# A fp32 decoder trunk on one core: weight tiles split once and kept in DRAM scratch, instead of split for every token group

## The chip, the core and the metric

The kernel runs on one core of a Trainium2 chip. The metric is the device time of one execution in microseconds (us). The engines are TensorE (PE), which multiplies matrices, VectorE (DVE), ScalarE (ACT), GpSimd (POOL), and SyncE (SP), from whose queue this kernel issues all of its DMAs, in order.

## The reference

One layer of a hybrid decoder trunk, for 2048 prompt tokens and 8 sample rows (one new token each for 8 sequences with state and caches), width 1024, all in float32. Cut to what matters:

```python
h    = rmsnorm(x, ln_mix)
proj = h @ w_in                      # 1024 x 3592
# A: gated DeltaNet, 4 heads x 128 (short convolution, chunked recurrence, gated norm) -> od
# B: dilated window attention, 8 heads x 64, three branches (window, dilation), ALiBi      -> oa
x    = x + concat(od, oa) @ w_out    # 1024 x 1024
h    = rmsnorm(x, ln_ffn)
x    = x + square(relu(h @ w_ffn_up)) @ w_ffn_down   # 1024 x 4096, 4096 x 1024
y    = rmsnorm(x, ln_final)
```

The outputs are y, the convolution's and the recurrence's last states, and the caches of keys and values, those of the samples shifted by one row (a copy of 64 MB).

## The kernel before, in words

**Dense products.** The 2056 tokens are worked in four groups (0 to 511, 512 to 1023, 1024 to 1535, and 1536 to 2055 in two pieces of 260). A float32 product is made of three: both operands are split, x = hi + lo with both parts in fp32r, and hi·hi, hi·lo and lo·hi are summed in PSUM (`dense`, L234, matmul at L244). A weight tile is 128 × 1024 floats (512 KB): 24 matmuls of 512 columns for a group (48 of 260 in the last). There are 100 such tiles: 28 of the input projection (`win`), 8 of the output projection (`wout`), 32 of the MLP's upper matrix (`wup`), 32 of its lower one (`wdn`). Each group goes through all of them, and the last takes 4 tiles of `wdn` twice, which makes 404 loads.

**A weight tile's way.** `load_w` (L219) issues the DMA of the raw tile from SP (L223), into a ring of `self.ahead` = 3 buffers; ACT copies it to `whi`, which rounds it (L216), and POOL subtracts that from the raw tile, which gives `wlo` (L217); `whi` and `wlo` have rings of three. When the mixers are done, `late` (L1474, called when the second group's MLP ends) opens a new pool of weights and sets `self.ahead` to 5.

**Order of the work.** First `in_proj` for the four groups, whose results are drained from PSUM by DVE and ACT, convolved, and stored to DRAM scratch from SP (`d_dn<-ct`, L382 and L390, for the recurrence's inputs; others for queries, keys and values). Then `ffn` (L1412): `out_proj` of the first group, and for each group the MLP, with the next group's `out_proj` before its last eighth. Beside the dense products run the *mixers*, a generator (`all_mixers`, L1266) which makes one step for every 10 dense products: recurrence inputs of the first half of the tokens (`delta_first(0)`, L527 to L569, each of 8 chunks ending in the PE line L569); the inverses of the recurrence's blocks (`dn_blocks`, L588 and L590, 31 steps of two DVE instructions for each half) beside the first half's attention; the scan over its chunks (`delta_scan(0)`, L627 to L729); then `delta_first(1)`, `dn_blocks(1)`, `attention(1)` (scores L840 and L866, transposes L822, products with the values L850 and L879, softmax on DVE L806 and ACT L810), `delta_scan(1)` and the sample rows. Before each `out_proj` the mixers are drained up to what it needs.

The program writes these as they come; a scheduler then sets each engine's fixed order, by priorities: what supplies the dense products first (lane "feed"), then the mixers, then the dense products (L31). The caches' copies (`copy_piece`, L1431, 128 of 512 KB, DRAM to DRAM) are spread over 300 weight tiles, from the 40th on. At the start the first group's tokens come as `xs`, are normed in parts (`s<-xs,cols`, L285), and the first row scale `rb` (L212) is made from their squares.

Of the kernel before, what the change touches and what calls it, by code (L numbers as in the profile page):

```python
# [7 lines left out]
F32 = mybir.dt.float32  # L8
# [8 lines left out]
T = 2048            # prompt tokens  # L17
NB = 8              # sample rows
TT = T + NB
# the token ranges of the dense products  # L20
GROUPS = (((0, 512),), ((512, 512),), ((1024, 512),), ((1536, 260), (1796, 260)))
# those of the first norm, the first group in parts so that the products start early
# [5 lines left out]
# weight tiles after which, and over which, the copies of the caches are spread  # L28
COPY_FROM, COPY_UNITS = 40, 300
COPY_LANE, COPY_LAG = 'mixer', 1  # L30
# dense products of 512 columns to a step of the mixers, beside the input projection and beside the MLP  # L31
STEPS = 10, 10
# blocks of queries between the scores and the turn, and between the turn and the products with the values
# [3 lines left out]
class Build:  # L37
    def __init__(self, nc, tc, ctx, I, O):
# [10 lines left out]
        self.pace = []  # L49
        self.units = -COPY_FROM  # L50
# [5 lines left out]
    # ---------------------------------------------------------------- helpers  # L56
    def stage(self, i):
        """Within a stage an engine prefers what keeps the dense products supplied, then the
        small products of the mixers, then the dense products, which fill what is left."""
        self.lanes = {k: 1000 + i * 1000000 + n * 300000 for n, k in enumerate(("feed", "mixer", "dense"))}  # L60
# [9 lines left out]
    def mix_step(self):  # L70
        """The next step of the mixers; TensorE takes it up after the dense products emitted so far."""
        with self.lane("mixer"), self.tc.issue_after(self.last), self.tc.issue_after(self.last_v):
            if next(self.mixers, None) is None:
                self.mixers = None

    def advance(self, products):
        """Called after so many dense products of 512 columns."""
        self.credit += products
        while self.credit >= self.step:
            self.credit -= self.step  # L80
            if self.mixers is not None:
                self.mix_step()

    def next_later(self):
        """A step of each generator of self.later, behind the dense products emitted so far."""
# [20 lines left out]
    def consts(self):  # L106
# [24 lines left out]
        # q is scaled by 1 / (8 slope) of its head, a power of two  # L131
# [5 lines left out]
    def scratch(self):  # L137
# [14 lines left out]
        self.d_s = dr.tile([16, 4096], F32, name="d_s")  # L152
        self.d_S = dr.tile([128, 512], F32, name="d_S")
# [11 lines left out]
    def rsqrt(self, y, v, t):  # L165
        """y = v ** -0.5 for v > 0."""
# [9 lines left out]
    def sumsq(self, x, n, k, tmp, tag):  # L176
        """Adds the squares of x, the k-th of eight tiles, to self.acc."""
# [9 lines left out]
    def rms_steps(self, out, n, tmp):  # L187
        """Leaves 1 / rms of n tokens in the rows of out, from self.acc. In steps."""
# [25 lines left out]
    def split(self, hi, lo, x, eng):  # L214
        """x = hi + lo, exactly up to the rounding of lo to float32r."""
# [3 lines left out]
    def load_w(self, src):  # L219
        nc, W = self.nc, self.W  # L220
        with self.lane("feed"):
            raw = W.tile([128, 1024], F32, name="wraw", bufs=self.ahead)
            ins = nc.sync.dma_start(raw, src)  # L223
            hi, lo = [W.tile([128, 1024], F32R, name=n) for n in ("whi", "wlo")]
            self.split(hi, lo, raw, nc.gpsimd)
# [8 lines left out]
    def dense(self, w, wo, hi, lo, off, n, p=None):  # L234
        """PSUM bank with sum_k w[k].T @ act[k][:, off:off+n]; both operands are split in two and the
        product of the low parts is below float32's last place."""
# [14 lines left out]
    # ---------------------------------------------------------------- input projection  # L251
    def norm1(self, g, X, nx):
        """Splits of x ln; the rows of rb hold 1 / rms of the tokens, by which the products are scaled. In steps."""
# [5 lines left out]
        for i, (c0, n) in enumerate(NORM1[g]):  # L259
# [10 lines left out]
            if g == 0:  # L270
                if i == 0:
                    self.w0 = [self.load_w(I["win"][4])]
# [4 lines left out]
                if i == 0:  # L277
                    self.w0 += [self.load_w(I["win"][u]) for u in (5, 6)]
# [4 lines left out]
    def norm_split(self, hi, lo, x, ln):  # L283
        """hi + lo = x ln"""
# [3 lines left out]
    def in_proj(self, g, following=None):  # L288
# [8 lines left out]
        for kind, j in order:  # L297
# [11 lines left out]
            else:  # L309
                units = [(self.load_w(I["win"][first[kind] + j]), j)]  # L310
            for c0, n in pieces:
                for w, i in units:
                    # the mixers' banks are free while the first scales are awaited
# [17 lines left out]
    def unit_ba(self, g, hi, lo):  # L331
        """Projections to beta and the decay: the weight's high part in columns 0..7, its low part in 32..39."""
# [21 lines left out]
    def silu2(self, y, n):  # L354
        """silu(2 y)"""
# [6 lines left out]
    def scaled(self, out, p, c0, n, scale=1.0):  # L362
        """out = p scale / rms of the tokens from c0"""
# [61 lines left out]
    def turn_values(self, y, j, c0, np_):  # L425
        """The values with the tokens on the partitions."""
# [18 lines left out]
    # ------------------------------------------------------- gates and DeltaNet  # L445
    def gate_math(self, pool, b, a, n, beta, g):
        """beta = sigmoid(b); g = -exp(a_log) * softplus(a + dt_bias); b, a: [128, n, 4] views."""
# [57 lines left out]
    def dn_first(self, c):  # L505
        """Everything of a chunk that does not depend on the state."""
# [11 lines left out]
        # decay[j, (h, i)] = exp(gc_i - gc_j) for i >= j, else 0  # L518
# [22 lines left out]
        # cc = beta / |k|^2, 1/|k| -> |k|  # L541
# [34 lines left out]
    def dn_blocks(self, half):  # L576
        """Inverses of the 32 x 32 unit upper triangular diagonal blocks, one block to a partition."""
# [18 lines left out]
    def dn_inverse(self, c, out):  # L596
        """Loads a chunk and completes the inverse of its unit upper triangular matrix."""
# [25 lines left out]
        # 32 -> 64  # L623
# [22 lines left out]
        # 64 -> 128  # L646
# [13 lines left out]
    def dn_scan(self, c, nak, x, u):  # L660
        """Takes the state through a chunk and leaves the chunk's outputs."""
# [75 lines left out]
    def together(self, *gens):  # L737
        """Runs generators side by side, a step of each at a time."""
# [32 lines left out]
    # ---------------------------------------------------------------- attention  # L771
    def attn_consts(self):
        nc, A = self.nc, self.A
        # -(distance in positions) of query p from key kk of (previous block, own block), -BIG outside the band
# [10 lines left out]
        # the widest branch: queries 64.. of each of two residues, keys 0..127 of its residue  # L785
# [6 lines left out]
        # row 6 part + 2 branch + head gives its value to the 64 rows of the head, for its branch  # L792
# [7 lines left out]
    def attn_softmax(self, j, b):  # L800
        """exp(score - max) of a block of queries for the two heads, with -max and the sums."""
# [11 lines left out]
    def attn_turn(self, b):  # L813
        """The block's probabilities with the keys on the partitions."""
# [17 lines left out]
    def attn_wide(self, hf, qd, i, qr, ks, so):  # L832
        """Scores of two residues of the widest branch."""
# [20 lines left out]
    def attn_near(self, br, hf, qd, i, parts, ks, so):  # L854
        """Scores of 128 queries of a near branch."""
# [27 lines left out]
    def attn_load(self, j, hf):  # L883
        """The queries of a head twice, its keys' high and low parts: (q, q) . (k high, k low) = q . k"""
# [41 lines left out]
    def attn_blocks(self, hf):  # L926
        """For each block of queries its scores, and what to do with its probabilities."""
# [59 lines left out]
    def attention(self, half):  # L987
        while self.have_at < 2 * half + 2:
            yield 1
        with self.pool(f"A{half}", 2, side="right") as self.A:  # L990
# [3 lines left out]
            while True:  # L994
                # a step: the products of one block, the turn of a later one, the scores of a still later one
# [16 lines left out]
    def attn_combine(self, j, t, s0, o):  # L1012
        """Weighs the branches' outputs for 512 tokens from t by their softmax denominators."""
# [6 lines left out]
        # e: exp(branch max - max), then the weights; columns 2 branch + head  # L1020
# [36 lines left out]
    # ---------------------------------------------------------------- sample rows  # L1057
    def sample_dn(self):
# [14 lines left out]
        # norms of q and k; kq[., bh, 0] = k, kq[., bh, 1] = q  # L1073
# [11 lines left out]
        # gates, the same on all partitions, in the order (b, h)  # L1085
# [9 lines left out]
        # state products  # L1095
# [446 lines left out]
```

## Time and profile before

| | us |
|---|---|
| median of 3 runs | 3205.29 (3204.25 to 3205.44) |
| span of the profiled execution | 3203.3 |
| PE, DVE, ACT, POOL busy | 2980.6, 2019.5, 1149.1, 1105.9 |
| start and the first of the input projection | 0 to 210 |
| rest of it, beside the first half's recurrence inputs and attention | 210 to 880 |
| first scan | 880 to 1160 |
| second half's inputs and block inverses, as the MLP of the first group goes on | 1160 to 1310 |
| second attention | 1310 to 1760 |
| second scan and the sample rows | 1760 to 2200 |
| dense products alone | 2200 to 3203 |

The span of the profiled execution is its own time from the first to the last recorded instruction; the median of the runs is 2.0 us above it. A line of the profile names a line of the code, the engine, the operation with its output and inputs, the shape, the count, the busy time, the mean of one in ns, and the engine's idle time before it with what ended it. The stages above have soft edges, since the mixers run beside the dense products.

### The profile page before, as it was taken

Reading aid. Unit: us, or ns where it says so; the run is one execution under the profiler, and the core shown is the slowest. Engines: PE = TensorE matmul, PEld = TensorE weight load, DVE = VectorE, ACT = ScalarE, POOL = GpSimd, SP = SyncE. Lnnn points to the kernel's source line nnn. Section 1 sums busy time; section 2 is a strip of 40 time slices with the busy share of each in tenths; the row PEclk is TensorE's granted clock in tenths of the full one; section 3 lists DMA queues with packets and bytes.
Section 4 is the critical chain, followed back from the end, with each engine's and each line's share of the span. In section 5 each row is a group of like instructions: output and inputs, shape, how many; then the busy total and the mean of one; then the engine's idle time right before and its main releaser. Section 6 shows DMA issues by size and latency. Waiting matters only on the chain.

```text
span 3203.3 us, 47999 instructions
## 1 busy us (share of the span) xinstructions
PE 2980.6 (93%) x17793; PEld 2489.5 (78%) x17793; DVE 2019.5 (63%) x4502; ACT 1149.1 (36%) x2298; POOL 1105.9 (35%) x557
## 2 busy tenths in 40 slices
PE   8898889999989889999999988979999999999997
PEld 6677667778988667677777767767888888999997
DVE  8658878657777687655546676685546344465545
ACT  4333335555523332344445332212233223332223
POOL 3333332232232234222223322424334444444443
PEclk9999999999989989999999988989999999999998
DMA  4555775455465665544444644675335444332222
GB/s 144 168 184 171 242 212 160 140 153 169 132 191 176 191 203 195 162 130 131 124 118 145 206 150 163 215 227 200 129 112 184 133 140 162 119 112 93 93 93 67
DMA packets 349321, 499.52 MB, mean 156 GB/s; under 512 B 74904, under 2 KB 247416, under 8 KB 343968
## 3 DMA queue, kind: packets, MB, share of 16 engines
q1 hardware_dynamic: 349088, 496.46, 50.4%
q8 instruction: 141, 2.31, 0.3%
q14 instruction: 92, 0.75, 0.1%
HBM read 414.61 MB, written 148.93 MB: 176 GB/s over the span
## 4 chain that ended last, share of the span: by engine, by line
PE 56%; DVE 12%; DMA 3%; issue 2%; ACT 1%; SPq 0%; POOL 0%; DVEq 0%; ACTq 0%; POOLq 0%
PE dense L244 44%; PE bank L866 2%; PE bank L822 2%; PE bank L879 1%; PE bank L840 1%; DVE y L1404 1%; PE bank L671 1%; DMA ak<-d_kl 1%; DVE s L1387 1%; DVE tmp L1386 1%; DVE dt L172 1%; DVE drr L173 1%; DVE racc L185 1%; PE bank L688 1%; PE bank L673 1%
## 5 line engine op out<-in xcount | busy, mean ns | idle before, releaser
L244 PE MATMUL dense<-s,whi 128*128 128x512 f32 (+2 forms) x8000 | 1702.6, 357 | 36.3 <-DVE y L1404 10.4
L217 POOL TENSOR_TENSOR wlo<-wraw,whi 128x1024 fp32r<-128x1024 f32 x404 | 979.7, 2425 | 1740.7 <-ACT whi L216 816.6
L244 PEld LDWEIGHTS dense<-s,whi 128*128 128x128 f32 x8000 | 1310.9, 192 | 252.5 <-issue 26.4
L244 PE MATMUL dense<-s,wlo 128*128 128x512 f32 (+2 forms) x4000 | 893.9, 356 | 0.0
L244 PEld LDWEIGHTS dense<-s,wlo 128*128 128x128 f32 x4000 | 664.3, 191 | 106.8 <-issue 6.5
L216 ACT ACTIVATE whi<-wraw 128x1024 fp32r<-128x1024 f32 x404 | 427.0, 1057 | 854.7 <-PE dense L244 707.7
L1404 DVE TENSOR_TENSOR y<-dense,y 128x512 f32<-128x512 f32 (+1 forms) x320 | 185.6, 583 | 295.5 <-PE dense L244 295.0
L1386 DVE TENSOR_TENSOR tmp<-tmp 128x512 f32<-128x512 f32 (+1 forms) x160 | 197.7, 1236 | 68.9 <-ACT s L1385 68.8
L810 ACT ACTIVATE as<-as,as 128x256 f32<-128x256 f32 (+2 forms) x384 | 169.9, 444 | 180.5 <-DVE as L806 170.9
L806 DVE CUSTOM_DVE_ANT_0 as<-bank,nd 128x256 f32<-128x256 f32 (+2 forms) x384 | 122.7, 349 | 160.9 <-PE bank L866 106.9
L1383 DVE SCALAR_TENSOR_TENSOR tmp<-dense,rb 128x512 f32<-128x512 f32 (+1 forms) x160 | 93.3, 583 | 172.7 <-PE dense L244 171.1
L1385 ACT ACTIVATE s<-tmp 128x512 fp32r<-128x512 f32 (+1 forms) x160 | 87.6, 548 | 292.1 <-DVE tmp L1383 290.7
L379 DVE SCALAR_TENSOR_TENSOR cy<-cr,cw,cy 128x512 f32<-128x512 f32 (+3 forms) x189 | 151.8, 804 | 12.2 <-ACT cy L377 10.1
L822 PE MATMUL bank<-ident,as 128*128 128x128 f32 (+1 forms) x600 | 112.1, 289 | 5.3 <-ACT as L810 4.0
L1387 DVE TENSOR_TENSOR s<-tmp,s 128x512 fp32r<-128x512 f32 (+1 forms) x160 | 107.6, 672 | 4.1
L822 PEld LDWEIGHTS bank<-ident,as 128*128 128x128 f32 (+1 forms) x600 | 65.0, 138 | 36.7 <-issue 17.8
L866 PE MATMUL bank<-ak,aql 128*128 128x256 f32 x256 | 88.2, 356 | 1.2 <-DVE aql L217 1.2
L866 PE MATMUL bank<-ak,aqh 128*128 128x256 f32 x256 | 88.4, 357 | 0.0
L358 ACT ACTIVATE ct<-cy 128x512 f32<-128x512 f32 (+3 forms) x83 | 44.1, 532 | 119.6 <-DVE cy L379 85.5
L827 DVE COPY apt<-bank 128x512 f32<-128x512 f32 (+2 forms) x96 | 55.3, 576 | 48.1 <-PE bank L822 43.9
L840 PE MATMUL bank<-ak,aq 128*64 128x64 f32 (+1 forms) x512 | 73.5, 374 | 12.7 <-issue 8.4
L879 PE MATMUL bank<-apt,av 128*64 128x128 f32 x944 | 82.9, 288 | 0.0
(343 smaller groups left out, 2871.7 us busy)
## 6 DMA issues: line engine op xcount, KB each, us to landing
wraw<-wdn SPq DMA_DIRECT2D x132, 512.0 KB, 3.6
wraw<-wup SPq DMA_DIRECT2D x128, 512.0 KB, 3.5
wraw<-win SPq DMA_DIRECT2D x112, 512.0 KB, 4.1
s_wk<-ck SPq DMA_DIRECT2D x64, 511.8 KB, 5.4
s_wv<-cv SPq DMA_DIRECT2D x64, 511.8 KB, 5.9
d_nak<-nak SPq DMA_DIRECT2D x16, 1024.0 KB, 4.8
nak<-d_nak SPq DMA_DIRECT2D x16, 1024.0 KB, 6.1
wraw<-wout SPq DMA_DIRECT2D x32, 512.0 KB, 3.9
```

The lines of the kernel that those rows point to most:

```text
L216: self.nc.scalar.activation(hi, x, AF.Copy)
L217: return eng.tensor_tensor(out=lo, in0=x, in1=hi, op=OP.subtract)
L244: self.last = nc.tensor.matmul(p[:, :n], a[:, wo + k * 128:wo + (k + 1) * 128], x[k][:, off:off + n], start=i == 0 and k == 0, stop=i == 2 ...
L379: nc.vector.scalar_tensor_tensor(y[:, :np_], r[:, i:i + np_], self.cw[:, j, i:i + 1], y[:, :np_], op0=OP.mult, op1=OP.add)
L806: nc.vector.tensor_tensor_reduce(out=st[:, hh, :nk], in0=b["s"][hh], in1=b["nd"], op0=OP.add, op1=OP.min, scale=-(2.0 ** -(2 * j + hh + 1) ...
L810: nc.scalar.activation(st[:, hh, :nk], st[:, hh, :nk], AF.Exp, bias=so[:, i, hh:hh + 1], scale=-1.0, accum_out=so[:, i, 2 + hh:3 + hh])
L822: nc.tensor.transpose(pT[:m, w * 128:(w + 1) * 128], b["p"][:, hh, kb * 128:kb * 128 + m], self.ident)
L866: nc.tensor.matmul(p[:, 256 * hh:256 * hh + 256], x[:, q], ks[hh][:, k], start=n == 0, stop=n == 1)
L879: self.nc.tensor.matmul(po[s64, 128 * i:128 * i + 128], v[:, own - (nkb - 1 - kb) * step, s64], b["pt"][:, hh * nkb + kb, :], start=kb == ...
L1386: nc.vector.tensor_tensor(out=u[:, :n], in0=u[:, :n], in1=u[:, :n], op=OP.mult)
L1387: nc.vector.tensor_tensor(out=ul[:, s], in0=u[:, :n], in1=uh[:, s], op=OP.subtract)
L1404: self.last_v = nc.vector.tensor_tensor(out=y[m][:, s], in0=p[:, :n], in1=y[m][:, s], op=OP.add).ins
```

## The change: the split tiles are kept

The parts of a weight tile are worked out when it is first needed (the first group), and stored to a DRAM scratch of 100 tiles of 1 MB, `d_w`. The other 304 loads bring both parts at once, by one DMA of 1 MB, and need neither ACT nor POOL. The two parts lie in one tile `w` with a ring of `self.ahead` buffers; the raw tile has a ring of 3.

```diff
+        self.kept = {}
...
+        self.d_w = dr.tile([100, 128, 2, 1024], F32, name="d_w")
...
-    def load_w(self, src):
+    def load_w(self, name, *i):
         nc, W = self.nc, self.W
+        again = (name, *i) in self.kept
+        k = self.kept.setdefault((name, *i), len(self.kept))
         with self.lane("feed"):
-            raw = W.tile([128, 1024], F32, name="wraw", bufs=self.ahead)
-            ins = nc.sync.dma_start(raw, src)
-            hi, lo = [W.tile([128, 1024], F32R, name=n) for n in ("whi", "wlo")]
-            self.split(hi, lo, raw, nc.gpsimd)
+            both = W.tile([128, 2, 1024], F32R, name="w", bufs=self.ahead)
+            hi, lo = both[:, 0], both[:, 1]
+            if again:
+                ins = nc.sync.dma_start(both.bitcast(F32), self.d_w[k])
+            else:
+                raw = W.tile([128, 1024], F32, name="wraw", bufs=3)
+                ins = nc.sync.dma_start(raw, self.I[name][i])
+                self.split(hi, lo, raw, nc.gpsimd)
+                nc.sync.dma_start(self.d_w[k], both.bitcast(F32))
...
-                units = [(self.load_w(I["win"][first[kind] + j]), j)]
+                units = [(self.load_w("win", first[kind] + j), j)]
```

The other callers name their tiles in the same way: ("wout", u), ("wup", f), ("wdn", c, m // 2). In the changed kernel a line stands 10 further down than before (2 further ahead of `load_w`): the matmul of the dense products is L254 there, the load of the kept parts L230, the raw load L233, the store L235.

The change also moves instructions, since the scheduler orders them anew. First PE, where the second attention begins. Before (`dense` are the dense products, L840 scores, L822 transposes of the probabilities, L850 products with the values):

```order
L244 MATMUL dense<-s,whi 128x512 x16
L244 MATMUL dense<-s,wlo 128x512 x6
L840 MATMUL bank<-ak_12809,aq_12808 64x128 x4
L244 MATMUL dense<-s,wlo 128x512 x2
L244 MATMUL dense<-s,whi 128x512 x16
L244 MATMUL dense<-s,wlo 128x512 x8
L244 MATMUL dense<-s,whi 128x512 x8
L244 MATMUL dense<-s,wlo 128x512 x4
```

Now, from the last chunk of the recurrence's inputs on (L537 to L579; L850 are the scores here, L832 the transposes, L860 the products with the values):

```order
L254 MATMUL dense<-s,w 128x512 x170
L537 MATMUL bank<-ident,dx 128x128 x4
L540 MATMUL bank<-ident,dx 128x128 x4
L563 MATMUL bank<-ident,dx 128x128 x4
L568 MATMUL bank<-dx 128x128 x4
L579 MATMUL bank<-dx 128x128 x4
L254 MATMUL dense<-s,w 128x512 x188
L850 MATMUL bank<-ak_12474,aq_12473 64x128 x4
L850 MATMUL bank<-ak_12480,aq_12479 64x128 x4
L832 MATMUL bank<-ident,as 128x128
L850 MATMUL bank<-ak_12474,aq_12473 64x128
L832 MATMUL bank<-ident,as 128x128
```

Before, 890 dense products stand among those of the second attention. Now none does: all of it stands in one piece behind them, and each chunk of the second half's recurrence inputs in one piece too, with 170 to 190 dense products between two chunks. Also four or five of the eight chunks of the first scan stand without dense products between them, where some 60 stood.

Next SP, in the input projection of a later group (`d_dn<-ct` is a store of a drained tile, the `nak` rows are stores of the recurrence's inputs). Before:

```order
L382 DMA d_dn<-ct 128x512
L223 DMA wraw<-win 128x1024
L574 DMA d_blk<-nak 32x4x32 x4
L571 DMA d_nak<-nak 128x2048
L382 DMA d_dn<-ct 128x512
L223 DMA wraw<-win 128x1024
L574 DMA d_blk<-nak 32x4x32
L382 DMA d_dn<-ct 128x512
L223 DMA wraw<-win 128x1024
```

Now:

```order
L392 DMA d_dn<-ct 128x512
L230 DMA w<-d_w 128x2048
L584 DMA d_blk<-nak 32x4x32 x3
L392 DMA d_dn<-ct 128x512
L584 DMA d_blk<-nak 32x4x32
L230 DMA w<-d_w 128x2048
L581 DMA d_nak<-nak 128x2048
L392 DMA d_dn<-ct 128x512
L230 DMA w<-d_w 128x2048
```

The rows alternate in the same way. What moved is which tile a load is for: before, the raw load of a tile stood behind the store of the drained product six or seven tiles earlier; now the load of the kept parts stands behind that of four tiles earlier, sometimes three.

Last ACT, at the start (L285 and L295 norm a part of the tokens, L184 and L186 square it, L212 and L214 make the row scale `rb`). Before:

```order
L216 ACTIVATE whi<-wraw 128x1024
L285 ACTIVATE s<-xs,cols 128x256
L184 ACTIVATE ct<-xs 128x256
L285 ACTIVATE s<-xs,cols 128x256
L184 ACTIVATE ct<-xs 128x256
L285 ACTIVATE s<-xs,cols 128x256 x8
L181 ACTIVATE racc<-xs 128x256
```

Now:

```order
L295 ACTIVATE s<-xs,cols 128x256
L186 ACTIVATE ct<-xs 128x256
L214 ACTIVATE rb<-fbank 128x256
L387 ACTIVATE cy<-cr,cw 128x256 x2
L218 ACTIVATE w<-wraw 128x1024
L295 ACTIVATE s<-xs,cols 128x256 x5
L183 ACTIVATE racc<-xs 128x256
```

The copy of the third weight tile, and the norm of the second half of the first tokens behind it, stand behind the first row scale now; before they stood ahead of it. On SP the first two stores of kept parts stand ahead of that half's loads.

More of the change, by code (lines that the diff above doesn't have):

```diff
@@ L271, in norm1 @@
                 if i == 0:
-                    self.w0 = [self.load_w(I["win"][4])]
+                    self.w0 = [self.load_w("win", 4)]
                 for k in range(8):
@@ L277, in norm1 @@
                 if i == 0:
-                    self.w0 += [self.load_w(I["win"][u]) for u in (5, 6)]
+                    self.w0 += [self.load_w("win", u) for u in (5, 6)]
             yield 1
@@ L1316, in out_proj @@
         for u in range(8):
-            w = self.load_w(I["wout"][u])
+            w = self.load_w("wout", u)
             with self.lane("feed"):
@@ L1375, in up @@
         g0 = GROUPS[g][0][0]
-        w = self.load_w(I["wup"][f])
+        w = self.load_w("wup", f)
         uh, ul = self.stile(), self.stile()
@@ L1399, in down @@
             if m % 2 == 0 and (c0 == g0 or (c == 7 and g == 3)):
-                w = self.load_w(I["wdn"][c, m // 2])
+                w = self.load_w("wdn", c, m // 2)
             s = slice(c0 - g0, c0 - g0 + n)
```

## The prediction

> **What bounds the kernel now.** I read the page's totals and its chain of waits first, then busy time by stretches of the span, then the waits of TensorE (PE) and of SyncE's queue (SP).
>
> ```profile
> span 3203.3 us, 47999 instructions
> PE 2980.6 (93%) x17793; PEld 2489.5 (78%) x17793; DVE 2019.5 (63%) x4502; ACT 1149.1 (36%) x2298; POOL 1105.9 (35%) x557
> ...
> PE 56%; DVE 12%; DMA 3%; issue 2%; ACT 1%; SPq 0%; POOL 0%; DVEq 0%; ACTq 0%; POOLq 0%
> ```
>
> PE is busy 93% of the span, so 3203.3 − 2980.6 = 222.7 us is all that is idle; after PE the chain goes by VectorE (DVE), and GpSimd (POOL) and ACT, whose weight work the change removes, hold hardly any of it themselves. The stretches (columns: us, then busy time and count of PE, PEld, DVE, ACT, POOL, then granted clock, DMA share, GB/s) show where the idle time lies:
>
> ```profile
> 0.00:210.00 210.00, 180.40 (x808) 147.22 (x809) 135.46 (x262) 81.06 (x133) 76.85 (x36) 0.95 0.53 162
> 210.00:880.00 670.00, 625.32 (x3864) 504.61 (x3863) 493.75 (x1351) 313.98 (x765) 204.93 (x108) 0.98 0.58 173
> 880.00:1160.00 280.00, 244.42 (x1866) 217.86 (x1865) 203.68 (x488) 90.98 (x195) 78.47 (x54) 0.91 0.61 183
> 1160.00:1310.00 150.00, 133.74 (x629) 107.05 (x628) 122.97 (x287) 39.13 (x53) 59.50 (x40) 0.97 0.59 194
> 1310.00:1760.00 450.00, 437.17 (x2633) 334.38 (x2632) 237.01 (x715) 213.87 (x561) 120.08 (x61) 0.99 0.49 134
> 1760.00:2200.00 440.00, 382.68 (x2110) 308.97 (x2110) 316.72 (x646) 110.97 (x195) 139.41 (x82) 0.91 0.59 188
> 2200.00:3203.00 1003.00, 976.89 (x5895) 869.42 (x5893) 509.94 (x759) 299.08 (x398) 426.66 (x181) 0.99 0.38 125
> ```
>
> PE is idle 45 us beside the first attention (210 to 880), 36 and 57 us beside the two scans (880 to 1160, 1760 to 2200), where the granted clock is 0.91, and only 13 us beside the second attention (1310 to 1760) and 26 us in the last third. The waits by name:
>
> ```profile
> PE bank L729 <- DVE dw L724: 50.4, 14, 6.5
> ...
> PE dense L244 <- ACT whi L216: 9.5, 3, 7.4
> ```
>
> The largest is a small product of the scan that waits for a DVE result. The dense products wait for a split weight 3 times, 9.5 us in all: weights are not what is late now.
>
> **The change part by part.** *What goes.* Of 404 weight tiles 304 are loaded ready-made.
>
> ```profile
> L217 POOL TENSOR_TENSOR wlo<-wraw,whi 128x1024 fp32r<-128x1024 f32 x404 | 979.7, 2425 | 1740.7 <-ACT whi L216 816.6
> ...
> L216 ACT ACTIVATE whi<-wraw 128x1024 fp32r<-128x1024 f32 x404 | 427.0, 1057 | 854.7 <-PE dense L244 707.7
> ```
>
> That is 304 × 2.425 = 737 us of POOL and 304 × 1.057 = 321 us of ACT. Both engines are idle some 2000 us, so by itself this is worth nothing. What it does to DVE is another matter. Two answers of the timeline, DVE's and POOL's, of the same moment (start, duration):
>
> ```profile
> 1292.31 0.39 DVE L590 TENSOR_TENSOR bu<-bu,bt 128x220 f32<-128x220 f32 x1
> 1292.73 2.60 DVE L588 TENSOR_TENSOR bt<-bn,bu 128x207 f32<-128x207 f32 x1
> 1295.37 0.37 DVE L590 TENSOR_TENSOR bu<-bu,bt 128x207 f32<-128x207 f32 x1
> ...
> 1292.72 2.39 POOL L217 TENSOR_TENSOR wlo<-wraw,whi 128x1024 fp32r<-128x1024 f32 x1 [6.11 <-ACT whi L216]
> ```
>
> A DVE instruction of 0.37 us lasts 2.60 us when it starts beside the subtraction: 2.2 us lost. The Trainium skill (SBUF — State Buffer, section "SBUF: two separate sides") says that the port pair shared by the two engines is an exclusive lock held for a whole instruction, its loser blocked; the trace agrees, 2.60 beside 0.37 us. The price lies between 0 (the subtraction falls into DVE's idle time) and 304 × 2.2 = 669 us of DVE time; DVE is busy 63%, so I take about half, some 330 us. Little of it bounds PE: it is 10% of the span, and the idle time before PE that DVE can end is that of the first attention and the two scans, 45 + 36 + 57 = 138 us. I take a third, **−45 us**, between −90 and −10.
>
> *Start.* The ACT order changes: the third copy and the later norm copies now stand behind the row scale.
>
> ```profile
> 14.69 1.04 ACT L216 ACTIVATE whi<-wraw 128x1024 fp32r<-128x1024 f32 x1
> ...
> 28.77 0.38 ACT L212 ACTIVATE rb<-fbank 128x256 f32<-128x256 f32 x1 [1.55 <-PE fbank L209]
> ```
>
> SP also has two stores, which wait for POOL, ahead of the second half of the tokens, so that half is normed later. The row scale stands 14 us behind this weight copy, the tokens' order in it is what shifts; where the products of the tiles at hand cover it, nothing is lost. From 0 to 12 us, about half taken: **+7 us**.
>
> *Stores.* 100 stores of 1 MB join the first group's loads. A store waits on SP for POOL's subtraction, and behind it stand the next loads of raw tiles and stores of the projection; but the raw loads waited for that subtraction before, too, for their slot. So the price is in the bytes.
>
> ```profile
> DMA packets 349321, 499.52 MB, mean 156 GB/s; under 512 B 74904, under 2 KB 247416, under 8 KB 343968
> ...
> q1 hardware_dynamic: 349088, 496.46, 50.4%
> ...
> s_wk<-ck SPq DMA_DIRECT2D x64, 511.8 KB, 5.4
> ...
> dx<-d_dn SPq DMA_DIRECT2D x16, 768.0 KB, 5.6
> ```
>
> ```profile
> 2240.00:2320.00 80.00, 80.00 (x346) 64.67 (x345) 39.62 (x45) 23.45 (x29) 31.71 (x14) 1.00 0.40 132
> 2400.00:2480.00 80.00, 80.00 (x353) 64.97 (x352) 51.10 (x65) 28.82 (x38) 37.93 (x16) 1.00 0.56 188
> ```
>
> At a share of 0.56 the engines moved 188 GB/s, so full they would move 188 / 0.56 = 336. In the first group's MLP a tile means 0.52 MB raw, 1.05 MB stored, a share of the cache copies (128 of 0.52 MB over 300 tiles, 0.22) and of the recurrence's traffic (8 chunks of 0.79 MB of dx and 1.05 MB of nak over some 52 tiles, 0.28): 2.07 MB, 6.2 us. A dense tile takes 24 × 80 / 346 = 5.55 us, and with a tenth of small products 6.15 us. DMA and PE come out level, so queueing decides: between 0 and 0.3 us on each of 100 tiles, **+10 us** (0 to 30). By the Trainium skill's measured 425 GB/s for one core (DMA: Bandwidth & Descriptors, section "Bandwidth") 2.07 MB would take an estimated 4.9 us, and this term would be 0.
>
> *Weights later.* Loads of the later groups go straight into a ring of three tiles (five in the last two groups), which a tile leaves only when its last product is done. Before, raw tiles ran ahead of that; now the lead is two tiles, 2 × 5.55 = 11.1 us, less the landing. SP, in order, has them behind stores of the projection (where it waits for DVE), and had waited for POOL instead.
>
> ```profile
> SPq L223 <- POOL wlo L217: 1481.6, 332, 22.9
> ```
> ```profile
> wraw<-wup SPq DMA_DIRECT2D x128, 512.0 KB, 3.5
> ...
> d_nak<-nak SPq DMA_DIRECT2D x16, 1024.0 KB, 4.8
> nak<-d_nak SPq DMA_DIRECT2D x16, 1024.0 KB, 6.1
> ```
>
> Nearest to a 1 MB load is the 1 MB of nak, 4.8 to 6.1 us, which leaves 5 us. So it is mostly covered; where SP stands behind a late store it isn't. **+8 us**, from 0 to 40 (304 tiles, one in ten 1.3 us late).
>
> *Second attention bare.* On PE the end of the recurrence's inputs and the second attention, spread among 890 dense products before, now stand bare behind them.
>
> ```profile
> L244 PE MATMUL dense<-s,whi 128*128 128x512 f32 x649 | 178.5, 406 | 0.0
> L244 PE MATMUL dense<-s,wlo 128*128 128x512 f32 x328 | 95.1, 408 | 0.0
> ```
> ```profile
> 1337.40:1374.60 37.20, 37.20 (x274) 27.97 (x273) 16.97 (x75) 22.66 (x75) 2.37 (x1) 1.00 0.47 136
> ```
>
> Between 1310 and 1760 us stand 649 + 328 = 977 dense products, 977 × 0.231 = 226 us, and so 2633 − 977 = 1656 small ones in some 217 us, 0.131 us each. Their work is the same; the price is the waits that nothing fills. The stretch of 37 us has 274 products of 0.136 us, so nearly all of them small, and PE is busy through all of it at full clock: 0 is the lower end inside the attention. At its start a chain is bare but for the 188 dense products ahead of it:
>
> ```profile
> 1256.92 4.31 DMA bn<-d_blk
> ...
> 1310.47 8.45 DMA ak<-d_kl
> ```
> ```profile
> L588 DVE TENSOR_TENSOR bt<-bn,bu x62: 190/372/2603, 416.3 to 1303.8; 128x31 f32<-128x31 f32 x4, 128x60 f32<-128x60 f32 x4, 128x87 f32<-128x87 f32 x4, 128x112 f32<-128x112 f32 x4
> ```
>
> A store near 4 us, this load of 4.3, 62 DVE steps of 0.37 (23 us, 35 with other DVE work between), a store again, then 8.45 for the keys: 45 to 60 us, beside 188 × 0.231 = 43. About 10 us are idle there, 5 more at each of three changes of heads, up to a tenth of 217 us for bare chains, and 10 us where the clock falls, as it did to 0.91 beside idle stretches: some 57 less the 13 us idle there before, **+45 us**, from 10 to 110 (a quarter of 217 us bare, and a chunk or two of recurrence besides).
>
> Sum: 3203.3 − 45 + 7 + 10 + 8 + 45 = 3228.3 us of span. The median of the runs (3205.29) is 2.0 us above this execution's span, so I add 2: **3230 us**.
>
> **Rivals.** *DVE's relief decides (faster).* Every removed subtraction that a DVE instruction of a chain now meets gives back the 2.2 us of the row. If the relief reaches its −90, the attention keeps PE full as in the 37 us row (+15), and the stores and start cost +12 and weights 3, the time is 3205 − 90 + 30 = 3145 to 3180 with less; I give **3172**. The Trainium skill's rule above, an exclusive lock, stands behind this rival. For it speaks that DVE is 82% busy beside the second blocks (122.97 of 150 us); against it, that it has to gain on PE, idle 7%.
>
> *The DMAs decide (slower by much).* The bytes rise from 499.52 MB by 100 × 1.05 written and 304 × 0.52 read, to 763. In this stretch the share is already 0.78 and PE loses its pace:
>
> ```profile
> 320.00:400.00 80.00, 66.64 (x340) 55.24 (x340) 64.97 (x161) 30.23 (x50) 29.76 (x18) 0.91 0.78 242
> ```
>
> If a tile's load comes later than the 5 us to spare (a landing above 11 us, or SP held 5 us by a store), each such tile shows it whole. With 100 of 304 tiles 0.6 us late (60) and the stores at +30, the time is 3230 + 52 + 20 = **3302**. Against: the share over the span would be only 50.4 × 763 / 499.52 = 77%.
>
> *Nothing to be measured.* Runs of this kernel lie within about 1 us; I call 0.2% (6.4 us) the least that can be told from no change. Relief at −65 and the rest as forecast give 3210.
>
> **How the numbers follow.** Forecast, slower by 0.2 to 2.5%: 0.40. Relief: 0.31. DMAs: 0.17. No change: 0.12. So faster 0.31, same 0.12, slower 0.57. Terms at their kind ends (−90, 10 and 0s) give 3125, at their bad ends (−10, 12, 30, 40, 110) 3387, which need not come together; a tenth left out on either side, the range goes from 3160 to 3310.
>
> **What would show it.** Right: DVE instructions of 2.6 us in the recurrence's steps are gone after the first group; PE has 30 to 80 us idle in the second attention; dense products wait for a weight load a few us in all, and where SP holds one back behind a projection's store. Wrong: PE idle under 20 us in the bare attention (then faster), or waits of dense products for the weight loads above 60 us (then slower).

## The result, and the profile after

The changed kernel takes 3226.47 us (median of 5 runs, 3223.65 to 3228.29), the kernel before in the same session 3205.29 (3202.89 to 3208.72): the ratio is 1.0061, 95% interval 1.0044 to 1.0077. It is slower by some 20 us, near the forecast of 3230. But that the sum came out right is luck: large errors of opposite sign in it cancelled, as the experiments show.

The page's totals after:

```profile
span 3221.5 us, 47130 instructions
PE 2969.5 (92%) x17793; PEld 2479.9 (77%) x17793; DVE 1707.0 (53%) x4502; ACT 834.6 (26%) x1994; POOL 365.3 (11%) x253
...
q1 hardware_dynamic: 363488, 760.71, 71.8%
```

DVE has 2019.5 − 1707.0 = 312 us less to do with the same 4502 instructions, POOL 741 and ACT 315 us less. PE is busy 11 us less, but idle 3221.5 − 2969.5 = 252 us instead of 223. The stretches, cut where PE's own stages end in this kernel (same columns as before):

```profile
0.00:240.00 240.00, 198.28 (x876) 158.65 (x877) 135.46 (x275) 83.97 (x139) 69.98 (x34) 0.94 0.76 272
240.00:876.00 636.00, 625.04 (x3833) 503.70 (x3831) 384.68 (x1346) 241.68 (x689) 33.54 (x37) 0.99 0.79 241
876.00:1215.00 339.00, 287.21 (x2037) 250.79 (x2036) 211.49 (x504) 89.42 (x194) 70.21 (x49) 0.91 0.77 246
1215.00:1530.00 315.00, 307.20 (x1413) 250.02 (x1411) 174.77 (x299) 79.48 (x102) 119.46 (x58) 1.00 0.88 302
1530.00:1592.00 62.00, 0.00 (x0) 0.00 (x1) 27.06 (x76) 1.26 (x2) 4.29 (x10) 0.53 1.06 295
1592.00:1860.00 268.00, 223.71 (x1656) 163.42 (x1656) 131.04 (x599) 149.91 (x487) 21.69 (x19) 0.86 0.37 90
1860.00:2335.00 475.00, 456.87 (x2527) 369.72 (x2528) 296.51 (x696) 74.16 (x165) 35.39 (x38) 0.98 0.79 266
2335.00:3221.00 886.00, 871.18 (x5461) 783.61 (x5459) 346.03 (x711) 114.72 (x216) 10.74 (x8) 0.99 0.63 223
```

Beside the first attention (240 to 876) PE is idle 11 us where it was 45, beside the second scan and the samples (1860 to 2335) 18 us at a clock of 0.98 where it was 57 at 0.91. Then one hole holds all of that and more: from 1530 to 1592 PE does nothing, and in the 268 us of the second attention, 1656 products without a dense one among them, it is idle 44 us at a clock of 0.86. The waits of PE name it:

```profile
PE bank L850 <- DMA ak<-d_kl: 85.7, 8, 62.5
PE bank L739 <- DVE dw L734: 36.6, 11, 5.7
PE dense L254 <- ACT w L218: 29.7, 11, 8.0
PE dense L254 <- DMA w<-d_w: 10.4, 6, 4.4
```

How the hole of 62.5 us comes about stands in two answers of the timeline. SyncE's (start, duration to issue), then DVE's:

```profile
1507.17 5.88 SPq L230 DMA_DIRECT2D w<-d_w  x2
1513.11 0.90 SPq L233 DMA_DIRECT2D wraw<-wdn  x2
1518.32 0.33 SPq L230 DMA_DIRECT2D w<-d_w  x1
...
1523.94 0.34 SPq L230 DMA_DIRECT2D w<-d_w  x1
1524.33 0.43 SPq L584 DMA_DIRECT2D d_blk<-nak  x1
1524.80 0.43 SPq L522 DMA_DIRECT2D dw<-d_gc  x1
...
1545.32 0.34 SPq L590 DMA_DIRECT2D bn<-d_blk  x1
...
1576.87 0.34 SPq L603 DMA_DIRECT2D d_u<-bu  x1
```
```profile
1529.93 0.69 DVE L529 TENSOR_TENSOR dw<-dw,gc 128x512 f32<-128x512 f32 x1 [16.50 <-DMA dw<-d_gc]
...
1553.50 0.20 DVE L598 TENSOR_TENSOR bt<-bn,bu 128x31 f32<-128x31 f32 x1 [19.76 <-DMA bn<-d_blk]
...
1559.41 0.39 DVE L598 TENSOR_TENSOR bt<-bn,bu 128x220 f32<-128x220 f32 x1
1559.83 0.39 DVE L600 TENSOR_TENSOR bu<-bu,bt 128x220 f32<-128x220 f32 x1
...
1576.62 0.19 DVE L600 TENSOR_TENSOR bu<-bu,bt 128x31 f32<-128x31 f32 x1
```

PE made the last chunk's products at 1485 us, and had 188 dense products after them:

```profile
1484.78 1.06 PE L579 MATMUL bank<-dx 128*128 128x128 f32 x8
```

The chunk's decays (`dw<-d_gc`) were issued only at 1524.80, behind the loads of ready tiles on SP, each of which waits for PE to leave its buffer, and behind two stores of kept parts ahead of those (issued at 1494.17 and 1499.67), which wait for POOL. Between 1483 and 1530 us SP stood about as long before the one kind as before the other:

```profile
SPq L230 <- PE dense L254: 16.9, 4, 5.2
SPq L235 <- POOL w L219: 16.3, 3, 7.4
```

So the chain began as the dense products ended: load, store, load of `bn` at 1545, the block inverses from 1553.5 to 1576.8, and the keys. The inverses' steps here last 0.19 to 0.43 us, none of them 2.6 us: there is no subtraction on POOL beside them.

### The profile page after: what moved, and what is told of

Same layout as the page of the kernel before. It is cut to its first block, busy times and chain, and to the rows that moved or that the text cites. A ratio compares the mean times of both kernels' runs of the same rounds, so it can differ in the third digit from the quotient of the medians.

```text
span 3221.5 us, 47130 instructions
## 1 busy us (share of the span) xinstructions
PE 2969.5 (92%) x17793; PEld 2479.9 (77%) x17793; DVE 1707.0 (53%) x4502; ACT 834.6 (26%) x1994; POOL 365.3 (11%) x253
## 3 DMA queue, kind: packets, MB, share of 16 engines
q1 hardware_dynamic: 363488, 760.71, 71.8%
## 5 line engine op out<-in xcount | busy, mean ns | idle before, releaser
L254 PE MATMUL dense<-s,w 128*128 128x512 f32 (+2 forms) x12000 | 2348.3, 354 | 58.2 <-ACT w L218 29.7
L254 PEld LDWEIGHTS dense<-s,w 128*128 128x128 f32 x12000 | 1938.9, 190 | 387.4 <-ACT w L218 33.1
L219 POOL TENSOR_TENSOR w<-wraw,w 128x1024 fp32r<-128x1024 f32 x100 | 241.0, 2414 | 435.9 <-ACT w L218 396.8
L1396 DVE TENSOR_TENSOR tmp<-tmp 128x512 f32<-128x512 f32 (+1 forms) x160 | 145.3, 908 | 81.1 <-ACT s L1395 81.1
L218 ACT ACTIVATE w<-wraw 128x1024 fp32r<-128x1024 f32 x100 | 105.7, 1058 | 289.8 <-issue 145.9
L850 PE MATMUL bank<-ak,aq 128*64 128x64 f32 (+1 forms) x512 | 72.3, 376 | 87.6 <-DMA ak<-d_kl 85.7
L389 DVE SCALAR_TENSOR_TENSOR cy<-cr,cw,cy 128x512 f32<-128x512 f32 (+3 forms) x189 | 135.8, 720 | 22.9 <-ACT cy L387 19.6
L850 PEld LDWEIGHTS bank<-ak,aq 128*64 128x64 f32 x512 | 46.4, 208 | 107.6 <-issue 99.9
L832 PE MATMUL bank<-ident,as 128*128 128x128 f32 (+1 forms) x600 | 122.6, 297 | 6.2 <-ACT as L820 5.2
L1064 POOL TENSOR_TENSOR ao<-ao,ao 128x512 f32<-128x512 f32 x32 | 41.4, 1293 | 627.8 <-ACT as L820 388.8
L876 PE MATMUL bank<-ak,aqh 128*128 128x256 f32 x256 | 101.5, 410 | 3.7 <-ACT ao L987 2.4
L832 PEld LDWEIGHTS bank<-ident,as 128*128 128x128 f32 (+1 forms) x600 | 70.6, 142 | 36.5 <-ACT as L820 13.9
L375 DVE SCALAR_TENSOR_TENSOR cy<-dense,rb 128x512 f32<-128x512 f32 (+1 forms) x60 | 34.9, 583 | 105.7 <-PE dense L254 90.8
```

Source lines behind the costliest of these rows:

```text
L218: self.nc.scalar.activation(hi, x, AF.Copy)
L219: return eng.tensor_tensor(out=lo, in0=x, in1=hi, op=OP.subtract)
L254: self.last = nc.tensor.matmul(p[:, :n], a[:, wo + k * 128:wo + (k + 1) * 128], x[k][:, off:off + n], start=i == 0 and k == 0, stop=i == 2 ...
L389: nc.vector.scalar_tensor_tensor(y[:, :np_], r[:, i:i + np_], self.cw[:, j, i:i + 1], y[:, :np_], op0=OP.mult, op1=OP.add)
L832: nc.tensor.transpose(pT[:m, w * 128:(w + 1) * 128], b["p"][:, hh, kb * 128:kb * 128 + m], self.ident)
L850: nc.tensor.matmul(p[64 * r:64 * r + 64, 256 * hh:256 * hh + nk], qr[hh][:, n:1024:16], ks[hh].bitcast(F32)[:, n:16 * nk:16], start=True, ...
```

## The experiments

Two theories stood against each other. **Order**: the removed subtractions are worth some 70 us (by the idle time above), and the stores on SP's queue, by moving the second attention out of the dense products, cost more than that. **Bytes**: the relief is small, and the 264 MB of added traffic are the cost.

**The relief alone.** On the kernel before; the low parts of 304 tiles (the 28 first and the 72 from the 112th on are split, which is the first group but for four tiles) are left out, ACT's copy stays. On PE the small products keep their places among the some 12000 dense ones, or shift by at most 16; the orders of SP and ACT shift in places too.

```diff
-            self.split(hi, lo, raw, nc.gpsimd)
+            if self.units + COPY_FROM < 28 or 112 <= self.units + COPY_FROM < 184:
+                self.split(hi, lo, raw, nc.gpsimd)
+            else:
+                nc.scalar.activation(hi, raw, AF.Copy)
+                lo = hi
```

> The kernel before, but the tiles of groups 2 to 4 are not subtracted: the high part stands in for the low one there, so their low parts are left out. Loads, copies on ACT and the order on PE stay those of before. If the removed subtractions free DVE and DVE then frees PE, the time falls by 55 to 85 us, to 3120 to 3150, and PE's waits for DVE in the scans and beside the first attention shrink. If the relief is worth nothing to PE (the changed kernel's gains came from its order or its loads), it stays within 10 us of 3205.

It took 3061.95 us, ratio 0.9543 (0.9527 to 0.9559): 146 us, well beyond the 85 that were the most expected. Its totals, two of its stretches and its longest wait:

```profile
PE 2935.5 (96%) x17793; PEld 2458.8 (80%) x17793; DVE 1694.3 (55%) x4502; ACT 1134.2 (37%) x2298; POOL 369.4 (12%) x253
```
```profile
210.00:836.00 626.00, 616.82 (x3891) 501.82 (x3890) 392.42 (x1358) 311.22 (x767) 33.88 (x38) 0.99 0.65 186
...
1702.00:2092.00 390.00, 374.84 (x2182) 305.55 (x2181) 257.66 (x653) 118.18 (x205) 26.30 (x34) 0.97 0.71 228
```
```profile
PE bank L733 <- DVE dw L728: 22.2, 11, 5.3
```

PE's idle time fell from 223 to 126 us, and its busy time by 45 us as well. Beside the first attention (3891 products here, 3864 before) it is 8.5 us less busy, beside the second scan and the samples 8 us less, with 72 products more in the stretch and the clock at 0.97 instead of 0.91. Idle time alone had undercounted what there was to win. The mean granted clock rose from 0.967 to 0.981, and busy time times clock is 2882 us before and 2880 here: the 45 us of busy time are the same products at a higher clock.

**The stores alone**, read by nobody, on the kernel before; and the same stores in the lowest lane of the priorities.

```diff
...
-            hi, lo = [W.tile([128, 1024], F32R, name=n) for n in ("whi", "wlo")]
+            both = W.tile([128, 2, 1024], F32R, name="w", bufs=3)
+            hi, lo = both[:, 0], both[:, 1]
             self.split(hi, lo, raw, nc.gpsimd)
+            if src.tensor.name + str(src.offset) not in self.kept:
+                self.kept[src.tensor.name + str(src.offset)] = len(self.kept)
+                nc.sync.dma_start(self.d_w[len(self.kept) - 1], both.bitcast(F32))
```

`self.kept` and `d_w` are set up as in the change. The second of the two issues the same store behind the block, in `with self.lane('dense')`.

> The kernel before, plus the 100 stores of split tiles from SP, which nobody reads; all 404 tiles are still loaded raw and split. If the stores put the second attention behind the dense products, PE has some 85 us more idle time there, and with 20 to 30 us more in the first group and no relief the time is 3290 to 3330. If the bareness came from the loads of ready tiles, or costs nothing in itself, this kernel is within 40 us of 3205.

3345.76 us, ratio 1.0429 (1.0405 to 1.0452): 138 us slower, beyond the range. The second attention stands bare on PE and its wait is there, so the stores do that, not the loads of ready tiles:

```profile
PE bank L846 <- DMA ak<-d_kl: 78.0, 11, 54.1
```

> The kernel before plus the 100 stores, as in the run of 3346 us, but in the lowest lane, so that the second attention stays among the dense products. If the place of the attention is the larger part of those 140 us, this one is at 3225 to 3270 (bytes and queue 20 to 60). If the bytes or SP's wait for POOL make the 140 us, it stays above 3320.

3268.75 us, ratio 1.019 (1.0174 to 1.0207). With the attention back among the dense products 77 of the 138 us are gone, and 61 are left. They stand in another wait:

```profile
PE dense L255 <- ACT w L218: 69.3, 21, 14.9
...
PE bank L851 <- DMA ak<-d_kl: 15.9, 7, 6.0
```

Dense products wait for a split weight, 9.5 us before, now 69.3. The raw loads are not what is late. A store reads the tile `w`, of which there are three, and the split that fills it anew has to wait until the store is done. By ACT's waits, late raw tiles ended 20 us of its idle time before the splits, stores 132 us. The longest wait of a dense product stands right behind such a split (ACT, then PE):

```profile
ACT w L218 <- DMA d_w<-w: 132.2, 36, 12.9
...
1209.59 1.06 ACT L218 ACTIVATE w<-wraw 128x1024 fp32r<-128x1024 f32 x1 [12.94 <-DMA d_w<-w]
...
1210.70 1.22 PE L255 MATMUL dense<-s,w 128*128 128x512 f32 x2 [14.87 <-ACT w L218]
```

With the stores in their first place no wait of a split is ended by a store, and dense products wait 29.5 us for split weights. So the lowest lane frees SP, and holds the tiles longer. Whether more buffers for `w` would win this back was not tried.

**The changed kernel with its stores in the lowest lane.**

```diff
-                nc.sync.dma_start(self.d_w[k], both.bitcast(F32))
+        if not again:
+            with self.lane('dense'):
+                nc.sync.dma_start(self.d_w[k], both.bitcast(F32))
```

> The changed kernel with its stores in the lowest lane of the scheduler's priorities; every byte is still moved, and the second attention stands among dense products again on PE. If the place of the attention was what cost 85 us, the time falls to 3125 to 3165, faster than both kernels. If the bytes are the cost (DMA share 0.87 beside the first group's MLP), it stays above 3195.

3166.93 us, ratio 0.9884 (0.9854 to 0.9913): faster than both kernels, 2 us above the range of the order theory; every byte is still moved, so the bytes alone do not make the changed kernel slower than the kernel before. Against the changed kernel that is, by the ratios, 57 us for one lane.

**Four of the 100 stores.** The later groups load these four tiles, 1 MB each time, and so multiply by wrong weights.

```diff
-                ins = nc.sync.dma_start(both.bitcast(F32), self.d_w[k])
+                ins = nc.sync.dma_start(both.bitcast(F32), self.d_w[k % 4])
...
-                nc.sync.dma_start(self.d_w[k], both.bitcast(F32))
+                if k < 4:
+                    nc.sync.dma_start(self.d_w[k], both.bitcast(F32))
```

> The changed kernel with 4 of its 100 stores; the later groups load 1 MB a tile as in the changed kernel, but of these four tiles, so they multiply by wrong weights. Against the kernel with the stores in the lowest lane this gives the price of 96 stores' bytes. If the stores cost what was forecast (+10, and +20 by the waits for the split parts), it is 10 to 30 us faster than that kernel, 3110 to 3145; if the bytes of the stores are the main cost, 60 us or more faster; if the loads of 1 MB are late, dense products wait for them by over 40 us in both.

3110.55 us, ratio 0.9691 (0.9669 to 0.9713). The 96 stores cost 56 us by the medians and 62 by the ratios, as the 100 did on the kernel before (61): twice and more what was forecast, at the edge of what the bytes' theory gave. Where they fall shows in the stretches of the first scan and the first chunks of the second half, with the stores in the lowest lane and with four of them:

```profile
891.00:1302.00 411.00, 325.77 (x2242) 284.17 (x2241) 271.07 (x704) 104.13 (x219) 79.46 (x64) 0.88 0.73 237
```
```profile
861.00:1239.00 378.00, 318.27 (x2244) 278.15 (x2243) 257.42 (x679) 104.55 (x220) 82.71 (x66) 0.91 0.66 206
```

The spans of these two executions differ by 53 us, and 33 of them lie here, in the same 2242 and 2244 products; 17 lie in the start. By PE's waits over the whole span, with all stores and then with four, dense products wait 31.8 and 11.6 us for split weights, and small products wait longer for their loads, most of all for the recurrence's inputs:

```profile
PE bank L539 <- DMA dx<-d_dn: 22.1, 8, 8.5
```
```profile
PE bank L538 <- DMA dx<-d_dn: 2.9, 3, 1.4
```

With all stores 27 splits wait 101.8 us for a store to be done; with four stores none does. So the 62 us are traffic and held buffers together, and how they divide stays open. The loads of 1 MB themselves are not late: dense products wait 11.9 us for them with four stores, 15.9 with all.

**Relief by contention, or by a shorter way?** The kernel of 3062 us, with POOL doing a subtraction of the same size that nobody waits for. PE and SP keep the order of that run.

```diff
                 nc.scalar.activation(hi, raw, AF.Copy)
+                nc.gpsimd.tensor_tensor(out=lo, in0=hi.bitcast(F32), in1=hi.bitcast(F32), op=OP.subtract)
                 lo = hi
```

> The kernel without the later groups' subtractions (3062 us), and in their place a POOL subtraction of the same size that reads the high part only, writes the idle low buffer, and that no instruction on PE, SP, DVE or ACT waits for; low parts are left out as there. If the relief was DVE no longer held up beside POOL, the held up DVE instructions of 2.6 us come back and with them the time: 3185 to 3215. If the relief was the shorter way of a weight (loads no longer queued on SP behind POOL), it stays at 3062 to 3085.

3165.57 us, ratio 0.9857 (0.9842 to 0.9872). Neither range held it: some 100 of the 146 us come back. Its totals and the added group:

```profile
PE 2971.9 (94%) x17793; PEld 2485.1 (79%) x17793; DVE 1969.4 (62%) x4502; ACT 1135.1 (36%) x2298; POOL 953.1 (30%) x557
```
```profile
L229 POOL TENSOR_TENSOR wlo<-whi 128x1024 fp32r<-128x1024 f32 x304 | 582.6, 1917 | 1329.9 <-ACT whi L228 1304.1 <-ACT egc L494 10.0 <-ACT rb L212 6.1
```

DVE has 275 of its 325 us back, from instructions of its own that did not change. So most of the relief is DVE no longer held up while POOL works. The Trainium skill (SBUF — State Buffer, section "SBUF: two separate sides") has the cause as a lock on a shared port pair; the trace agrees with it here a second time, 275 us of DVE's time for 304 instructions of POOL. This subtraction lasts 1.92 us where the real one lasts 2.43, and the order differs a little from that of before, so the remaining 46 us are not all the shorter way of a weight; how they divide stays open.

**The copies of the caches.** SP issued 24 of them between 1490 and 1600 us, around the hole of 62.5 us. First the changed kernel, then the one with low stores, with the copies begun at the 180th tile.

```diff
-COPY_FROM, COPY_UNITS = 40, 300
+COPY_FROM, COPY_UNITS = 180, 210
```

> The changed kernel as it is, but with the copies of the caches begun at the 180th weight tile; the second attention stays bare. Its longest wait, 62.5 us for the keys ahead of the second attention, had 24 copies on SP and a DMA share of 1.06. If the copies lengthen that chain, the wait falls to 45 to 52 us and the time to 3195 to 3220. If the chain itself (stores, block inverses on DVE, loads) makes it, it stays at 58 us or more and the time within 8 us of 3226.

3224.2 us, ratio 1.0045 (1.0027 to 1.0063), against 1.0061 without this edit: no difference that can be told. The wait fell to 54.5 us, between the two theories' numbers:

```profile
PE bank L850 <- DMA ak<-d_kl: 78.0, 8, 54.5
```

So the copies are some 8 us of the hole, and the chain itself is the rest.

> The changed kernel with its stores in the lowest lane (3167 us), and with the copies of the caches begun at the 180th weight tile instead of the 40th, after the first group's stores. The stores cost that kernel 56 us against the one with 4 stores. If that was DMA traffic crowding (stores and copies at once), the time falls by 10 to 35 us, to 3132 to 3157. If it was SP's queue or the split parts' own waits, it stays at 3160 to 3175. If the copies crowd the later loads, it rises above 3175.

3151.01 us, ratio 0.981 (0.9788 to 0.9831): as expected of crowding, below the run without the later copies by 16 us by the medians and 24 by the ratios. It is the fastest kernel here that computes all of the reference, 1.9% faster than the kernel before.

**The loads off SP's queue.** With four stores and with ready tiles the kernel is still 47 us above the one without subtractions. A ready tile's load waits on SP for PE, and the mixers' DMAs wait behind it. In the scheduled order, the first attention begins some 330 dense products earlier if these loads are on POOL's queue.

```diff
-                ins = nc.sync.dma_start(both.bitcast(F32), self.d_w[k])
+                ins = nc.gpsimd.dma_start(both.bitcast(F32), self.d_w[k])
```

The first of three runs has this in the kernel with four stores (`k % 4` in place of `k`), the second in the kernel of 3151 us; the third has the stores on POOL's queue as well, right behind their subtractions.

> The changed kernel with 4 stores, the later groups loading these four tiles (3111 us), but with their loads issued from POOL's queue instead of SP's; the weights are wrong as there. On SP a load of a ready tile waits for PE to leave its buffer, 978 us in all in the changed kernel, and the mixers' DMAs stand behind it; in PE's order the first attention begins some 330 dense products earlier without that. If this queueing is what the loads cost (3111 against 3062 us without subtractions), the time falls to 3055 to 3090. If the 1 MB loads are dear by their bytes or landing, it stays at 3100 to 3125.

> The changed kernel with the stores in the lowest lane and the copies from the 180th tile on (3151 us), and the loads of ready tiles issued from POOL's queue. If SP's queueing is what these loads cost, the time falls by 30 to 60 us, to 3090 to 3120. If it is their bytes, it stays at 3140 to 3160.

> The changed kernel with the stores and the loads of ready tiles issued from POOL's queue, and the copies from the 180th tile on. A store then stands right behind the subtraction that it waits for, and holds up nothing on SP. If the stores cost by SP's queue, the time falls further than with the loads alone, to 3065 to 3100; if by their bytes, it is that of the loads alone within 12 us; if descriptors issued by POOL hold up DVE or each other, it is above 3130.

They took 3284.52 (ratio 1.0241, 1.0214 to 1.0267), 3365.17 (1.049, 1.0461 to 1.052) and 3362.96 us (1.0491, 1.0453 to 1.0529), the first two far above both of their ranges. The third lies 2 us from the second and above 3130, which its expectation had for the stores' bytes and for descriptors issued by POOL, but neither can be read from it. The edit had undone something else: the copies were paced by standing behind the loads on SP, and lost that. In the first of the three, 74 copies went out between 119 and 337 us:

```profile
119.00:337.00 218.00, 115.54 (x468) 92.22 (x467) 53.58 (x93) 36.36 (x57) 36.34 (x19) 0.76 1.02 303
```

With the DMA engines full, PE was idle half of the time. These three tell nothing on SP's queue, nor on whether POOL's is dear. So, in the second of these kernels, the copies went to POOL's queue too (`nc.gpsimd.dma_start` in `copy_piece`):

> The run with the loads of ready tiles on POOL's queue took 3365 us, but the copies of the caches had lost the loads that paced them and stood in a heap on SP: 75 of them between 100 and 460 us, with the DMA engines full. Here the copies are issued from POOL's queue as well, spread among the loads as in the kernel of 3151 us, from which it differs by the queue of loads and copies alone. If SP's queueing behind the loads is what they cost, the time is 3090 to 3125. If the loads cost by their bytes, it is 3140 to 3160. If DMAs from POOL's queue are dear in themselves, it is above 3165.

3213.45 us, ratio 1.0014 (0.9992 to 1.0036), 62 us above the kernel with both on SP by the medians, in the range for "dear in themselves". The queue theory is not borne out in this form. But what is dear need not be the DMAs: POOL now waits in SP's place, and its own instructions for the mixers stand behind the loads:

```profile
POOL w L230 <- PE dense L256: 1516.0, 274, 23.3
```

Whether the 47 us are queueing on an in-order queue, whichever it is, or something else, and what makes POOL's queue the worse one, stays open.

## Why the prediction was right, and where it was not

By the ratios, the change is a chain of four: −146 us (subtractions gone), +47 (ready tiles loaded by 1 MB, with the order that comes of it), +62 (96 stores in the lowest lane: their traffic, and the tiles that they hold), +57 (the stores' lane, which moves the second attention): +20.

- **DVE's relief, forecast −45 (−90 to −10): −146.** This is the step that failed most. That DVE would have some 330 us less to do was right (325 and 312). But I held that "little of it bounds PE", and bounded the gain by a third of the 138 us of idle time that DVE can end. PE's idle time fell by 97 us and its busy time by 45 in the run of the relief alone. Of the 97, some 84 lie in the three stretches of the 138 us, where I had taken a third; the 45, the same products at a higher granted clock, the sum did not have at all.
- **Stores, forecast +10 (0 to 30): +61 and +62 in two pairs.** Bytes over a mean rate against PE's time for a tile came out level, and I took a tenth of a microsecond a tile. The rate held (302 GB/s at a share of 0.88 from 1215 to 1530 us in the changed kernel would be 343 at a full share; 336 was taken). What was missing is that a store keeps its tile from being filled again (dense products wait 69.3 us for split weights where this was measured alone), and that PE waits longer for the mixers' loads beside the stores (22.1 us instead of 2.9 for `dx`).
- **Second attention bare, forecast +45 (10 to 110): +57 and +77 in two pairs.** These prices are those of the lane as a whole. The place, the chain and the wait for the keys were right. The cover was not: I let 188 dense products (43 us) run beside the chain, and the whole of it came after them, because SP held a load of 256 KB behind stores and loads of weights. So the hole is 62.5 us, and not about 10. (The small products' 217 us of the working should read 437 − 226 = 211, which changes its terms by about 1 us.)
- **Weights later, +8 (0 to 40):** dense products wait 10.4 us for `w<-d_w`, as forecast. The 47 us between the kernel with four stores and that without subtractions are more than this; some of them are order, and they are not settled.
- **Start, +7 (0 to 12): about 1.** PE has made 876 products at 222 us before, 877 at 223 with four stores, and 876 at 240 with all of them (quoted above), so the 17 us belong to the stores. The first stretch of the kernel before and of the one with four stores:

```profile
0.00:222.00 222.00, 192.40 (x876) 157.24 (x877) 142.75 (x271) 87.80 (x144) 81.95 (x38) 0.95 0.54 166
```
```profile
0.00:223.00 223.00, 190.69 (x877) 154.82 (x878) 145.70 (x274) 83.50 (x140) 70.23 (x35) 0.97 0.61 194
```

- **Rivals.** "DVE's relief decides" had the mechanism and even too small a price; what ate it was the stores, twice over: by their lane, and by being there at all. "The DMAs decide" had a share of 77%; it is 71.8%, and loads of ready tiles are nearly never late. Its stores at +30 were half of the true price.

The signs that were named came: the 2.6 us instructions are gone from the inverses, and dense products wait a few us for ready tiles. PE's idle time in the second attention with its start is 106 us, above the 30 to 80 named.

## What to carry to other kernels

Take what an edit removes out by itself once, with everything else in place: the idle time of the engine that sets the end was no bound for it here, since its granted clock rose as its waits went, and its busy time fell too, by about half as much. And a store that waits for a result on an in-order queue is not free because nobody waits for the store: try the lowest place among what that queue carries, since here that place alone was worth 57 to 77 us. Then look at what waits for the buffer that the store reads: here 27 and 36 splits did, in the two kernels with low stores. Where work is said to be hidden beside other work, follow each small load of its chain on its queue before counting the cover.

## What was not expected of the hardware

- A POOL subtraction whose two inputs are the same tile takes 1.92 us, with two tiles 2.43 us (128 × 1024, same output type). The one reads `whi` as float32, the other as fp32r, so which of the two differences makes it is not shown.
- With fewer waits PE's granted clock was higher: 97 us less idle time came with a mean of 0.981 instead of 0.967, and so with 45 us less busy time for the same 17793 instructions.
- A DMA of 1 MB issued by POOL takes 0.53 us of POOL's time, 162.5 us for 304:

```profile
L230 POOL DMA_DIRECT2D w<-d_w x304 | 162.5, 535 | 1703.3 <-PE dense L255 1581.4
...
w<-d_w POOLq DMA_DIRECT2D x304, 1024.0 KB, 5.2
```

  Its median to landing, 5.2 us in that run, lies in the range that was read from the 1 MB of `nak` (4.8 to 6.1).
